# A 128-byte tile ahead of the MLP pool, one rotation step bound to VectorE, and a short VectorE pause at the second half of the token turns

## The chip, the cores and the metric

One Trainium2 chip (trn2), one core of it. The metric is device time in microseconds (us) for one execution of the whole program; the kernel before takes 616.29 us (median of three runs, 615.42 to 616.64). The engines are named as the profile names them: PE (TensorE matmul) and PEld (its weight load), DVE (VectorE), ACT (ScalarE), POOL (GpSimd), SP (SyncE, which issues most transfers).

## What is computed

A two-layer decoder trunk on 256 tokens of width 1024, in float32:

```
for layer in range(2):
    hn = rms_norm(h, gain[layer, 0])
    h = h + (stick_breaking_attention(hn) if layer == 0 else nsa_attention(hn, shared))
    h = h + square(relu(rms_norm(h, gain[layer, 1]) @ w1)) @ w2      # 1024 -> 4096 -> 1024
    if layer == 0:
        shared = nsa_shared_kv(h)        # compressed, selected and window keys and values
return rms_norm(h, final_norm)
```

Layer 0 attends over all earlier tokens with stick-breaking weights. Layer 1 is a native sparse attention: 16 query heads in four groups read compressed blocks, selected blocks and a window, mixed by sigmoid gates. A partial rotary embedding turns the first 16 of each head's 64 query dimensions; the rotated queries are needed for two of the three branches.

## The kernel before, in words

**Precision.** A float32 product is made of three matmuls: each operand is held as a high part (type fp32r) and a low part, and `mm3` (on top of `mm`, whose line is L443) adds high times high, high times low and low times high. For every weight tile of 128x1024 that lands in `raw`, ACT casts it to `wh` (L356) and DVE subtracts to get `wl` (L371). These two are made on the fly for nearly every weight, six buffers deep, and are the largest work of ACT and DVE. In a matmul the first operand in the code is the stationary one (loaded by PEld), the second the moving one (streamed). The names in a profile row stand as moving, stationary.

**Stages.** `layer0` (attention A), `mlp` for layer 0, `layer1` (shared keys and values, queries, sparse attention, output projection), `mlp` for layer 1, then the final norm. Each stage's private tiles live in a tile pool of its own (`ap`), opened by `scoped` at the same place in SBUF; long-lived tiles, the weight buffers (`wp`) and the slots that stages share (`cp`) lie below it.

**MLP.** `mlp` walks the 4096 hidden columns in 16 chunks of 256. For each half of a chunk, `first` multiplies the tokens with w1 into a bank `pu` (eight matmuls of 512 columns with `wh` stationary, eight of 256 with `wl` stationary; the tokens `xn` move). `square` makes the squared ReLU in `ms`, casts it to `hh` (L650) and subtracts to get `hl` (L651). Two chunks later `half` multiplies with w2 into seven accumulators `acc` (512 columns each; here `hh` or `hl` is stationary and the weight moves). Six chunks of each layer use a scheme with fewer products, for which DVE forms sums of weight tiles (`ty`) that are split like the weights into `th` and `tl`; those then move in place of `wh` and `wl`. `ms`, `hh`, `hl`, `th` and `tl` are the tiles of the MLP pool.

**Token turns.** Ahead of each MLP the residual `hres` is transposed on PE into two banks `pt` (`xt_turn`), eight token blocks in two halves of four. `xt_evac` takes each block out: ACT writes the high part of `xn` (L504), DVE the low part (L505). `first` needs block k before its k-th matmul. The second half is turned inside `mlp`, after the first quarter of the first chunk's matmuls.

**Queries of layer 1.** `q_proj` projects one of four groups into a bank `qp`. ACT copies it to `qu` (L1233), DVE multiplies by the cosine table into `qm` (L1234) and shuffles `qu` into `qw` (L1236); then `qw` is multiplied by the sine table (L1237 on POOL or L1238 on DVE) and added to `qm` (L1239 or L1240).

**What sets the order.** PE's instructions stand as the code emits them. The order on DVE, ACT and POOL is made while the kernel is built, by the class `Order`: a planner with its own clock that advances with every matmul. Work comes as chains of steps, each with a rank and, for every engine that may take it, a planned cost. When the planner thinks that an engine is free, it gives it the ready step of lowest rank. `rank_of` gives weight splits 0.5, 2 or 4 by how soon they are used. `quiet` makes an engine take no step of rank 2 or more for a planned time. On the chip each engine then runs its list strictly in order, and waits on semaphores.

**Addresses.** The build gives these tiles the following first bytes in every partition (several buffers of one name differ by 4096, 4608 or 8192 bytes, or by multiples of them, so one stands for all; `xn` has two places):

| tile | role in matmuls | first byte | remainder by 256 |
| --- | --- | --- | --- |
| `wh`, `wl` | moving or stationary | 98208, 122784 | 160 |
| `xa`, `xn`, `xk`, `xq`, `oT` | moving or stationary | 16032 or 49056 | 160 |
| `hh`, `hl` | stationary | 165408, 177696 | 32 |
| `th`, `tl` | moving | 189984, 206368 | 32 |
| `wgs` (layer 1, gate weights) | stationary | 157536 | 96 |

Of the kernel before, what the change touches and what calls it, by code (L numbers as in the profile page):

```python
# [8 lines left out]
F32 = mybir.dt.float32  # L9
# [6 lines left out]
P = 128  # L16
D = 1024
# [141 lines left out]
def act(n, f, more=0):  # L159
    return {"A": (195 + 0.835 * n + more, f, False)}  # L160


def dve(n, f, more=0, port=False):
    return {"D": (150 + 1.045 * n + more, f, port)}
# [7 lines left out]
def hybrid_kernel(ctx, tc, x, xt, eye, gcols, gfin, wqk, wv, wo0, wkv, wvs, wq, wg, wo1, w1, w2, cw1, cw2, cpos, gate_b, consts, out):  # L172
    nc = tc.nc
# [7 lines left out]
    o = Order()  # L181

    def go(gen, rank=1, lag=LAG):
        return Chain(o, gen, rank, o.now + lag)
# [3 lines left out]
    def f32(a):  # L188
        return a.bitcast(F32)

    def slot(i, shape, dt, name):
        return cp.tile(shape, dt, tag=f"e{i}", name=name, bufs=1)
# [4 lines left out]
    def B(i, name, dt=F32):  # L197
        return ps.tile([P, 512], dt, tag=f"b{i}", name=name, bufs=1)
# [215 lines left out]
    def W(i, part=None):  # L414
        if i > ws.cur:
            ws.cur = i
            for q in range(i, min(i + 4, len(items))):
                for c in ws.parts[q] or ():
                    c.hurry(rank_of(q))
        while any(ws.parts[q] is None for q in range(i + 1)):  # L420
            o.run(o.run(o.t))
        for p in range(items[i][3]) if part is None else (part,):
            for q in range(items[i][4] + p + 1):
                c = ws.parts[home[q]][q - items[home[q]][4]]
                if not c.done:
                    c.hurry()
            o.need(ws.parts[i][p])
        return ws.raws[items[i][2][0]] if items[i][0] == "r" else ws.made[i]

    def gone(x):  # L430
        for i in x if isinstance(x, list) else [x]:
            assert ws.gone == i, (ws.gone, i)
            ws.gone += 1
            if items[i][0] == "r":
                used(items[i][2][0])
        now, ws.waiting = ws.waiting, []
        for w in now:
            o.at(o.now, w.finish)
# [10 lines left out]
    def mm3(o_, a, b, first, last):  # L449
        mm(o_, a[0], b[0], first, False)  # L450
        mm(o_, a[0], b[1], False, False)
        mm(o_, a[1], b[0], False, last)

    def tr(o_, a, i, rate=2.0):
        nc.tensor.transpose(o_, a, i)  # L455
        o.tick(a.shape[0] / 2.4 * rate + 3)
# [4 lines left out]
    def both(xt_, k):  # L461
        return xt_[0][:, k, :], xt_[1][:, k, :]

    def cut(hl, a, b):
        return hl[0][:, a:b], hl[1][:, a:b]
# [30 lines left out]
    def xt_banks(banks):  # L496
        return [B(banks[b], f"pt{b}").rearrange("p (j q) -> p j q", j=2) for b in range(2)]

    def xt_evac(pt, j, b, half, gi, xt_, rank=0.5):
        k = 4 * half + 2 * b + j  # L500
        g = gc[:, gi * NK + k:gi * NK + k + 1]

        def one():
            yield act(256, lambda: nc.scalar.activation(xt_[0][:, k, :], pt[b][:, j, :], AF.Copy, scale=g), 60)  # L504
            yield dve(256, lambda: nc.vector.scalar_tensor_tensor(  # L505
                xt_[1][:, k, :], pt[b][:, j, :], g, f32(xt_[0][:, k, :]), op0=OP.mult, op1=OP.subtract), 60)
        return go(one(), rank)

    def xt_turn(pt, half, gi, xt_):
        ch = []  # L510
        for b in range(2):
            for j in range(2):
                k = 4 * half + 2 * b + j
                for t in range(T):
                    tr(pt[b][:, j, t * P:(t + 1) * P], hres[t][:, k * P:(k + 1) * P], ident)
            ch += [xt_evac(pt, j, b, half, gi, xt_) for j in range(2)]
        return ch
# [35 lines left out]
    def mlp(layer, gi, x_, ch, pt, rs, pus, accs, extra, mid, order, ends, ap):  # L553

        ws.tp = ap
        mus = slot(1, [P, 2, 2, 512], F32, "mu")
        mu = [mus[:, i] for i in range(2)]
        wa, wb = i_m[layer]
# [42 lines left out]
        def begin(c):  # L601
            return ([B(pus[c % 2][f], f"pu{f}") for f in range(2)] if c < 4 else [None, None],
                    (mu[c % 2], ap.tile([P, 9, P], F32, name="ms")), [])
# [70 lines left out]
            first(0, st[0], f, 0, NK // 2)  # L674
        gone(wa[0][0])
        o.need(*rs)
        ch.extend(xt_turn(pt, 1, gi, x_))
        st.append(begin(1))
        for f in range(2):
# [315 lines left out]
    def layer1(xk, pt0, ch, ap):  # L995
# [63 lines left out]
        def kv_proj(n, banks, mid=None):  # L1059
            pk = [B(b, "pk") for b in banks]  # L1060
            for k in range(NK):
                if k == 4 and mid is not None:
                    mid()
                if n == 0 and k == 2:
                    o.need(*nxt[2], *nxt[3])
                    pt1 = xt_banks((6, 7))
                    ch.extend(xt_turn(pt1, 1, 4, xk))
                    rc.extend([go(rstd_of(t, rstd), 0.8) for t in range(T)])
                    for half in range(2):
                        for b in range(2):  # L1070
                            for j in range(2):
                                qc[4 * half + 2 * b + j] = xt_evac((pt0, pt1)[half], j, b, half, 2, xq, 2.5)
                w = W(i_kv[n][k // 4][k % 4 // 2])
                if n == 0:
                    o.need(ch[k])
                for t in range(T):
                    mm3(pk[t], tok(xk, k, t), cut(w, k % 2 * 512, (k % 2 + 1) * 512), k == 0, k == NK - 1)
                if k % 2:
                    gone(i_kv[n][k // 4][k % 4 // 2])
            o.need(*rc)  # L1080
            for t in range(T):
                if n == 0:
                    kd0c.append(go(first_out(t, pk[t])))
                else:
                    krope[t] = go(key_out(t, pk[t]), 0.9)
# [125 lines left out]
        def q_proj(g, b, k0=0, k1=NK):  # L1211
            if k0 == 0:
                qps[g] = B(b, "qp")
            qp = qps[g]
            for k in range(k0, k1):
                w = W(i_q[g][k // 4])
                for j in range(2):
                    c = k % 4 * 256 + j * P
                    o.need(qc[k])
                    mm3(qp[:, j * 256:(j + 1) * 256], cut(w, c, c + P), both(xq, k), j == 0 and k == 0, k == NK - 1)  # L1220
                if k % 4 == 3:
                    gone(i_q[g][k // 4])
            if k1 < NK:
                return

            def gen():
                u = ap.tile([P, 2, T * P], F32, name="qu", bufs=3)
                m = ap.tile([P, 2, T * P], F32, name="qm", bufs=3)
                s = ap.tile([P, 2, T * P], F32, name="qw")
                src = qp.rearrange("p (j q) -> p j q", j=2)  # L1230
                tab = [rbc_[:, i, None, :].to_broadcast([P, 2, T * P]) for i in range(2)]
                yield rbc
                yield [act(512, lambda: nc.scalar.copy(u, src), -35),  # L1233
                       dve(512, lambda: nc.vector.tensor_mul(m, src, tab[0]))]  # L1234
                qu[g] = u
                yield dve(512, lambda: nc.vector.stream_shuffle(s, u, swap), 50)  # L1236
                yield {"G": (1040, lambda: nc.gpsimd.tensor_mul(s, s, tab[1]), True),  # L1237
                       "D": (690, lambda: nc.vector.tensor_mul(s, s, tab[1]), True)}  # L1238
                yield {"G": (1260, lambda: nc.gpsimd.tensor_add(m, m, s), True),  # L1239
                       "D": (690, lambda: nc.vector.tensor_add(m, m, s), True)}  # L1240
                qs[g] = m
            qch[g] = go(gen(), 0.8)

        qps, pvs = {}, {}
# [322 lines left out]
        pt = xt_banks((6, 7))  # L1567
# [10 lines left out]
    def scoped(f, name, *a, bufs=2):  # L1578
        with tc.tile_pool(name=name, bufs=bufs, reuse_waits="tile") as ap:
            return f(*a, ap)  # L1580

    x1, ch, pt, rs = scoped(layer0, "l0")
    nxt = {}

    def to_nsa(i, t, n, q, c):
# [3 lines left out]
        if i == 2:  # L1589
# [3 lines left out]
            nxt["ch"] = xt_turn(nxt["pt"], 0, 4, nxt["x"])  # L1593

    scoped(mlp, "m0", 0, 1, x1, ch, pt, rs, ((4, 5), (6, 7)), (0, 1, 2, 3), (4, 5, 6), to_nsa, ((0, 0), (1, 0), (1, 1), (0, 1)), [[(0, 512)]] * 4)
    x1, ch, pt, rs = scoped(layer1, "l1", nxt["x"], nxt["pt"], nxt["ch"], bufs=1)
    gf = slot(0, [P, D], F32, "gf")
# [6 lines left out]
    def finish(i, t, n, q, c):  # L1604
# [37 lines left out]
        last[t].append(go(gen(), 0.2))  # L1642

    scoped(mlp, "m1", 1, 3, x1, ch, pt, rs, ((2, 3), (6, 7)), (0, 1, 4, 5), (2, 3, 6), finish, ((0, 0), (1, 1), (0, 1), (1, 0)), ends)
    o.need(*last[0], *last[1])

# [103 lines left out]
```

## Time and profile before

| | |
| --- | --- |
| runs | 615.42, 616.29, 616.64 us; median 616.29 |
| the profiled execution | 616.42 us, of which the trace's span is 614.6 us |
| granted TensorE clock | 0.997 of full |
| PE busy | 604.0 us (98%), 3544 instructions |
| DVE, ACT, POOL busy | 507.2 us (83%), 377.1 us (61%), 40.6 us (7%) |
| chain that ended last | PE 90%, DVE 5%, DMA 2%, ACT 1%, issue 1% |
| DMA | 108.30 MB, mean 176 GB/s |

How to read it. A matmul's own length in a row (392 ns for 512 columns) is not what it costs, because matmuls overlap; what one costs is the distance from its start to the next start, or the length of a merged piece in the chain of waits divided by its count. "Idle before" stands in brackets in a timeline row, with what ended it. The stages lie at about 0 to 112 us (layer 0's attention), 112 to 288 (its MLP), 288 to 431 (layer 1's shared parts, queries, attention and projection), 431 to 606 (its MLP) and the last 8 us (the final norm's tail).

### The profile page before, as it was taken

Reading aid. Unit: us, or ns where it says so; the run is one execution under the profiler, and the core shown is the slowest. Engines: PE = TensorE matmul, PEld = TensorE weight load, DVE = VectorE, ACT = ScalarE, POOL = GpSimd, SP = SyncE. Lnnn points to the kernel's source line nnn. Section 1 sums busy time; section 2 is a strip of 40 time slices with the busy share of each in tenths; the row PEclk is TensorE's granted clock in tenths of the full one; section 3 lists DMA queues with packets and bytes.
Section 4 is the critical chain, followed back from the end, with each engine's and each line's share of the span. In section 5 each row is a group of like instructions: output and inputs, shape, how many; then the busy total and the mean of one; then the engine's idle time right before and its main releaser. Section 6 shows DMA issues by size and latency. Waiting matters only on the chain.

```text
span 614.6 us, 9427 instructions
## 1 busy us (share of the span) xinstructions
PE 604.0 (98%) x3544; PEld 507.7 (83%) x3544; DVE 507.2 (83%) x743; ACT 377.1 (61%) x623; POOL 40.6 (7%) x57
## 2 busy tenths in 40 slices
PE   8999999999999999999999999999999999999994
PEld 5899988888888888888887888677888888888884
DVE  6669996699889888986837999673997988988885
ACT  6757665566666566664806876462866756656642
POOL 0000000000000000000112442310000000000000
PEclk9999999999999999999999999999999999999998
DMA  8984444274574666565556544223656456465501
GB/s 313 394 275 138 138 134 137 75 262 158 179 245 148 210 203 191 186 231 170 173 170 206 174 145 163 69 70 103 213 164 228 149 193 235 155 209 202 172 0 70
DMA packets 31582, 108.30 MB, mean 176 GB/s; under 512 B 3888, under 2 KB 5168, under 8 KB 31536
## 3 DMA queue, kind: packets, MB, share of 16 engines
q1 hardware_dynamic: 30960, 107.07, 52.2%
q8 instruction: 28, 0.46, 0.3%
q10 hardware_dynamic: 576, 0.62, 0.3%
q14 instruction: 18, 0.15, 0.1%
HBM read 106.63 MB, written 1.05 MB: 175 GB/s over the span
## 4 chain that ended last, share of the span: by engine, by line
PE 90%; DVE 5%; DMA 2%; ACT 1%; issue 1%; POOL 0%; SPq 0%; POOLq 0%; ACTq 0%; DVEq 0%
PE acc L443 35%; PE pu L443 29%; PE qk L443 8%; PE pk L443 4%; PE pv L443 3%; PE po L443 3%; PE z L443 2%; PE qp L443 2%; DVE wl L371 2%; PE ph L443 1%; DMA raw<-in_wq 1%; PE pt L455 1%; PE pa L455 1%; DMA rv<-in_wv 1%; PE ptp L455 1%
## 5 line engine op out<-in xcount | busy, mean ns | idle before, releaser
L371 DVE TENSOR_TENSOR wl<-raw,wh 128x1024 fp32r<-128x1024 f32 (+1 forms) x180 | 210.0, 1190 | 30.9 <-ACT wh L356 29.4
L356 ACT CAST wh<-raw 128x1024 fp32r<-128x1024 f32 (+1 forms) x180 | 180.2, 1025 | 63.5 <-issue 23.2
L443 PE MATMUL pu<-xn,wh 128*128 128x512 f32 x512 | 129.8, 392 | 0.0
L443 PEld LDWEIGHTS pu<-xn,wh 128*128 128x128 f32 x512 | 94.8, 188 | 20.1 <-issue 0.5
L443 PE MATMUL acc<-wh,hl 128*128 128x512 f32 x196 | 77.1, 394 | 0.0
L443 PE MATMUL acc<-wh,hh 128*128 128x512 f32 x196 | 76.9, 393 | 0.0
L443 PE MATMUL acc<-wl,hh 128*128 128x512 f32 x196 | 76.9, 392 | 0.0
L443 PEld LDWEIGHTS pu<-xn,wl 128*128 128x128 f32 x512 | 70.8, 190 | 5.8
L443 PE MATMUL pu<-xn,wl 128*128 128x256 f32 x512 | 72.6, 282 | 0.0
L630 ACT COPY mu<-pu 128x512 f32<-128x512 f32 x64 | 37.3, 583 | 20.8 <-PE pu L443 20.8
L443 PE MATMUL qk<-xa,wh 128*128 128x256 f32 x256 | 47.3, 286 | 0.0
L650 ACT CAST hh<-ms 128x512 fp32r<-128x512 f32 x64 | 34.1, 553 | 16.4 <-DVE ms L646 12.9
L443 PE MATMUL acc<-wh,oT 128*128 128x512 f32 x128 | 43.6, 402 | 0.5 <-DVE oT L533 0.5
L443 PEld LDWEIGHTS acc<-wh,hl 128*128 128x128 f32 x196 | 36.8, 188 | 8.4
L443 PEld LDWEIGHTS acc<-wh,hh 128*128 128x128 f32 x196 | 37.1, 189 | 6.3
L443 PEld LDWEIGHTS acc<-wl,hh 128*128 128x128 f32 x196 | 36.9, 188 | 6.3
L356 ACT CAST th<-ty 128x1024 fp32r<-128x1024 f32 x24 | 25.2, 1051 | 26.2 <-DVE ty L390 13.8
L443 PEld LDWEIGHTS qk<-xa,wh 128*128 128x128 f32 x256 | 39.8, 192 | 0.5 <-issue 0.3
L651 DVE TENSOR_TENSOR hl<-ms,hh 128x512 fp32r<-128x512 f32 x64 | 37.3, 600 | 0.2 <-ACT hh L650 0.2
L443 PE MATMUL qk<-xa,wl 128*128 128x256 f32 x128 | 36.2, 283 | 0.0
L1276 ACT ACTIVATE pe<-z,nm 128x256 f32<-128x256 f32 (+1 forms) x64 | 26.3, 430 | 13.4 <-DVE nm L1282 10.2
L443 PE MATMUL pk<-wh,xk 128*128 128x512 f32 (+1 forms) x128 | 33.6, 342 | 0.0
(202 smaller groups left out, 949.2 us busy)
## 6 DMA issues: line engine op xcount, KB each, us to landing
raw<-in_w SPq DMA_DIRECT2D x128, 512.0 KB, 4.8
raw<-in_wqk SPq DMA_DIRECT2D x16, 512.0 KB, 5.8
raw<-in_wo SPq DMA_DIRECT2D x16, 512.0 KB, 4.2
raw<-in_wkv SPq DMA_DIRECT2D x8, 512.0 KB, 4.8
raw<-in_cw SPq DMA_DIRECT2D x8, 512.0 KB, 4.5
raw<-in_wq SPq DMA_DIRECT2D x8, 512.0 KB, 6.0
rv<-in_wv SPq DMA_DIRECT2D x6, 512.0 KB, 6.9
raw<-in_wvs SPq DMA_DIRECT2D x4, 512.0 KB, 5.7
```

What stands on the lines that cost most here:

```text
L356: k = {"A": (195 + 0.835 * m, lambda: nc.scalar.copy(a, b), False), "D": (200 + 0.49 * m, lambda: nc.vector.tensor_copy(a, b), True)}
L371: yield {"D": (150 + 1.045 * m, lambda: nc.vector.tensor_sub(lo, raw, f32(hi)), True)}
L443: nc.tensor.matmul(o_, a, b, start=first, stop=last, skip_group_check=True)
L455: nc.tensor.transpose(o_, a, i)
L630: yield act(512, lambda: nc.scalar.copy(u[:, f, :], pu[f]))
L650: yield act((b - a) * P, lambda: nc.scalar.copy(hh[:, into], flat[:, q]))
L651: yield dve((b - a) * P, lambda: nc.vector.tensor_sub(hl[:, into], flat[:, q], f32(hh[:, into])), port=True)
L1276: return act(n, lambda: nc.scalar.activation(d, z, AF.Exp, bias=nm[:, i:i + 1], accum_out=rs[:, t, hd, b:b + 1]), 150)
```

## The change

Four edits, of which the second and the last act on the same place:

1. `mlp` first allocates an unused tile of 128 bytes per partition, so that `ms`, `hh`, `hl`, `th` and `tl` all start 128 bytes later. Their remainder by 256 becomes 160, that of the other matmul operands.
2. `xt_evac` gets rank 0.3 instead of 0.5 where no rank is given.
3. In `q_proj` the multiplication by the sine table may no longer go to POOL for the last group (g = 3).
4. In `mlp`, just before the second half of the token turns, `quiet("D", 2200)` keeps DVE free of steps of rank 2 or more for 2200 planned ns.

```diff
-    def xt_evac(pt, j, b, half, gi, xt_, rank=0.5):
+    def xt_evac(pt, j, b, half, gi, xt_, rank=0.3):
...
         ws.tp = ap
+        ap.tile([P, 32], F32, name="pad", bufs=1)
         mus = slot(1, [P, 2, 2, 512], F32, "mu")
...
         o.need(*rs)
+        o.quiet("D", 2200)
         ch.extend(xt_turn(pt, 1, gi, x_))
...
-                yield {"G": (1040, lambda: nc.gpsimd.tensor_mul(s, s, tab[1]), True),
-                       "D": (690, lambda: nc.vector.tensor_mul(s, s, tab[1]), True)}
+                turned = {"G": (1040, lambda: nc.gpsimd.tensor_mul(s, s, tab[1]), True),
+                          "D": (690, lambda: nc.vector.tensor_mul(s, s, tab[1]), True)}
+                yield turned if g < 3 else {"D": turned["D"]}
```

PE's order, its shapes and its operands are the same before and after, and so is SP's order of transfers. What moves is on DVE, ACT and POOL, in three places.

DVE at the second half of the token turns in layer 1's MLP, before (`xn` rows are the low parts of four token blocks; `wl_4481` and `wl_4496` belong to the third chunk, `wl_4412` and `wl_4471` to the first two):

```order
L371 TENSOR_TENSOR wl_4412<-raw_4008,wh_4411 128x1024
L371 TENSOR_TENSOR wl_4471<-raw_4022,wh_4470 128x1024
L371 TENSOR_TENSOR wl_4481<-raw_4233,wh_4480 128x1024
L371 TENSOR_TENSOR wl_4496<-raw_4244,wh_4495 128x1024
L505 SCALAR_TENSOR_TENSOR xn_4417<-pt0_4447,gc_70,xn_4417 128x256 x2
L505 SCALAR_TENSOR_TENSOR xn_4417<-pt1_4448,gc_70,xn_4417 128x256 x2
L371 TENSOR_TENSOR wl_4513<-raw_4363,wh_4512 128x1024
```

The same place after the change (numbers of buffers have moved by one or two):

```order
L371 TENSOR_TENSOR wl_4413<-raw_4009,wh_4412 128x1024
L371 TENSOR_TENSOR wl_4473<-raw_4023,wh_4472 128x1024
L505 SCALAR_TENSOR_TENSOR xn_4418<-pt0_4448,gc_70,xn_4418 128x256 x2
L505 SCALAR_TENSOR_TENSOR xn_4418<-pt1_4449,gc_70,xn_4418 128x256 x2
L371 TENSOR_TENSOR wl_4483<-raw_4234,wh_4482 128x1024
L371 TENSOR_TENSOR wl_4498<-raw_4245,wh_4497 128x1024
L371 TENSOR_TENSOR wl_4514<-raw_4364,wh_4513 128x1024
```

Two weight splits have moved from ahead of the four `xn` steps to behind them. In layer 0's MLP one split moves in the same way. Some later steps of the third and fourth chunk change places with their neighbours in layer 1 (the difference `ms` of 256 columns, its cast and its subtraction go behind a weight split or two); a few rows further on the lists are the same again.

DVE at the last query group, before (`sct` is a step of the compressed branch, `nm` the row maxima of the next head pair, `oT` the attention output that the projection needs):

```order
L1236 STREAM_SHUFFLE qw_3985<-qu_3983 128x512
L371 TENSOR_TENSOR wl_3989<-raw_3799,wh_3988 128x1024
L1240 TENSOR_TENSOR qm_3984<-qm_3984,qw_3985 128x512
L533 TENSOR_TENSOR oT_3991<-po_3992,oT_3991 128x512
L1282 TENSOR_REDUCE nm_4037<-z1_4024 128x2
L1282 TENSOR_REDUCE nm_4037<-z1_4025 128x2
L1422 TENSOR_TENSOR sct_4050<-psc_4044,cst_74 128x256
```

The same place after the change:

```order
L1238 STREAM_SHUFFLE qw_3986<-qu_3984 128x512
L371 TENSOR_TENSOR wl_3990<-raw_3800,wh_3989 128x1024
L1240 TENSOR_TENSOR qw_3986<-qw_3986,rbc_2940 128x512
L1243 TENSOR_TENSOR qm_3985<-qm_3985,qw_3986 128x512
L533 TENSOR_TENSOR oT_3992<-po_3993,oT_3992 128x512
L1285 TENSOR_REDUCE nm_4038<-z1_4025 128x2
L1285 TENSOR_REDUCE nm_4038<-z1_4026 128x2
L1425 TENSOR_TENSOR sct_4051<-psc_4045,cst_74 128x256
```

DVE has one step more, between the split and the addition (lines after the change stand one to three higher). POOL's list loses that step, `L1237 TENSOR_TENSOR qw_3985<-qw_3985,rbc_2939 128x512`, and nothing else.

## The prediction, as it was written before the changed kernel ran

> **What bounds the kernel now.** I read the page's shares first, then the chain of waits.
>
> ```profile
> span 614.6 us, 9427 instructions
> PE 604.0 (98%) x3544; PEld 507.7 (83%) x3544; DVE 507.2 (83%) x743; ACT 377.1 (61%) x623; POOL 40.6 (7%) x57
> PE 90%; DVE 5%; DMA 2%; ACT 1%; issue 1%; POOL 0%; SPq 0%; POOLq 0%; ACTq 0%; DVEq 0%
> ```
>
> The end is set by PE: it is never long idle, and 90% of the chain is its own work. So only two things shorten the run: a smaller distance between matmuls, or a stall of PE taken away. The 5% of DVE are such stalls, nearly all in layer 1's attention.
>
> A matmul's distance is read from merged pieces of the chain (start, length, what; length divided by count). In order of time: 256-column matmuls of layer 0, one steady round of layer 0's MLP (two chunks), then three later places.
>
> ```profile
> 28.40 14.39 PE qk L443 x120
> ...
> 179.89 2.09 PE acc L443 x9
> 181.98 2.77 PE pu L443 x16
> 184.75 2.77 PE acc L443 x12
> 187.53 2.77 PE pu L443 x16
> 190.29 2.77 PE acc L443 x12
> 193.07 2.77 PE pu L443 x16
> 195.83 2.79 PE acc L443 x12
> 198.62 2.81 PE pu L443 x16
> ...
> 294.87 13.65 PE pk L443 x60
> ...
> 326.03 1.85 PE gp L443 x8
> ...
> 411.43 5.49 PE acc L443 x24
> ...
> 460.84 5.58 PE acc L443 x24
> ```
>
> A 256-column matmul takes 119.9 ns (14.39/120). The four `pu` pieces hold 32 matmuls of 512 and 32 of 256 columns in 11.12 us, so one of 512 takes (11.12/32) - 0.120 = 227.6 ns. `pk` takes 227.5 ns. But the four `acc` pieces of the same round hold 45 matmuls in 10.42 us: **231.6 ns**, and the 24 at 460.84 take 232.5. They have the same columns and types, and like `pk` the moving weights `wh` and `wl`. What differs is the stationary tile: `hh` and `hl`, at remainder 32 by 256 in the address table, where `pu` and `pk` have only tiles at 160. Two more pieces fit this. `gp` has a stationary tile at 96 and takes 231.3 ns. The 24 at 411.43 are also called `acc`, but their stationary tile is `oT` at 160: 228.8 ns, a restart behind a transposition included.
>
> **Part 1, the pad.** It moves `hh`, `hl`, `th` and `tl` to 160. How many matmuls touch them, from the groups by form (the first group stands three times with the same count, for `hh`, `hl` and both weight parts; the second too):
>
> ```profile
> L443 PE MATMUL acc<-wh,hl 128*128 128x512 f32 x194 | 76.6, 395 | 0.0
> L443 PE MATMUL acc<-th,hl 128*128 128x512 f32 x48 | 18.9, 394 | 0.0
> ```
>
> 3 x 194 + 3 x 48 = 726. (The 12 of 256 columns at the end gain nothing that I count.) If each falls from 231.6 to the 227.6 of its neighbours `pu`, that is 4.0 ns x 726 = **2.9 us**. Upper end: from the 232.5 of the piece at 460.84 to 227.5, 5.0 x 726 = 3.6 us. Lower end while the address is the cause: to the 228.8 of `oT`, 2.8 x 726 = 2.0 us. If it is not the cause: 0, or less than nothing (rivals). I take 2.9, since `pu` runs in the same rounds beside the same DVE and ACT work.
>
> One thing speaks against the words "share one remainder". `th` and `hh` share one already, 32:
>
> ```profile
> 153.76 0.40 PE L443 MATMUL acc<-wh,hl 128*128 128x512 f32 x1
> 154.00 0.40 PE L443 MATMUL acc<-th,hh 128*128 128x512 f32 x1
> ...
> 155.39 1.78 PE L443 MATMUL pu<-xn,wh 128*128 128x512 f32 x7
> ```
>
> Six matmuls with `th` or `tl` moving in 1.39 us are 231.7 ns each, no less than the mixed ones, and the step from `wh` to `th` took 240. So equality alone does not bring 227.6; 160 together with 160 does. That is enough here, since the change brings all to 160.
>
> The Trainium skill says otherwise: "TensorE: Matmul & The Clock Gate", section "Step-by-step: what each phase is for", gives PE two independent read ports of SBUF, one for the streamed operand and one for weights, and "SBUF — State Buffer", section "SBUF: two separate sides", lets PE wait on nobody. By that rule no start address would cost time, and this part would give 0 (the first rival's sum). The rows of `gp` and `acc` speak against it; that the address is the cause no run here shows yet.
>
> DVE and ACT also read and write the shifted tiles. I count nothing: DVE's subtraction takes 683 ns on `hl` (all at 32) and 679 on `wl` (all at 160).
>
> ```profile
> L651 DVE TENSOR_TENSOR hl<-ms,hh 128x512 fp32r<-128x512 f32 x44 | 30.0, 683 | 0.2 <-ACT hh L650 0.2
> L371 DVE TENSOR_TENSOR wl<-raw,wh 128x512 fp32r<-128x512 f32 x12 | 8.2, 679 | 0.0
> ```
>
> Can the rest follow a faster PE? In the next round (stretch, its length, then busy us of PE, PEld, DVE, ACT, POOL) DVE works 19.27 of 21.53 us, so it has 2.26 free; PE would gain 45 x 4 ns = 0.18. It can.
>
> ```profile
> 201.43:222.96 21.53, 21.53 (x110) 18.27 (x110) 19.27 (x25) 13.68 (x19) 0.00 (x0) 1.00 0.60 196
> ```
>
> **Part 2, the rotation on DVE.** The timeline at the last query group:
>
> ```profile
> 383.76 1.21 DVE L371 TENSOR_TENSOR wl<-raw,wh 128x1024 fp32r<-128x1024 f32 x1
> ...
> 383.95 2.15 POOL L1237 TENSOR_TENSOR qw<-qw,rbc 128x512 f32<-128x512 f32 x1 [3.58 <-DVE qw L1236]
> ...
> 386.13 0.69 DVE L1240 TENSOR_TENSOR qm<-qm,qw 128x512 f32<-128x512 f32 x1 [1.16 <-POOL qw L1237]
> 386.28 0.66 PE L455 MATMUL ptp<-ident,pe 128*128 128x128 f32 x4
> 386.74 0.68 DVE L533 TENSOR_TENSOR oT<-po,oT 128x512 fp32r<-128x512 f32 x1
> ...
> 387.48 0.50 PE L443 MATMUL acc<-wh,oT 128*128 128x512 f32 x1 [0.54 <-DVE oT L533]
> ```
>
> POOL needs 2.15 us, DVE stands idle for 1.16 of it, and behind the waiting addition stands the `oT` subtraction that PE waits for. After the change DVE does the multiplication itself, at the 0.69 us of the addition, which has the same shape. The split ends at 384.97, so the addition starts at about 385.68 instead of 386.13, and `oT` comes 0.45 earlier, at 386.97 instead of 387.42. PE's four transpositions are done at 386.94 (386.28 + 0.66), so PE can take that: **0.45 us**. What comes next on DVE (row maxima, `sct`) feeds ACT and PE in turn and moves along with it. Upper end: PE's whole wait, 0.54. Lower end: 0, if the next wait is not DVE's; below nothing only if POOL was a help, and it was what all waited for.
>
> **Part 3, rank and pause.** The timeline in layer 1's MLP:
>
> ```profile
> 432.61 4.62 DVE L371 TENSOR_TENSOR wl<-raw,wh 128x1024 fp32r<-128x1024 f32 x4
> ...
> 434.66 1.57 ACT L504 ACTIVATE xn<-pt,gc 128x256 fp32r<-128x256 f32 x4 [0.34 <-PE pt L455]
> ...
> 436.31 1.08 PE L443 MATMUL pu<-xn,wh 128*128 128x512 f32 x4
> ...
> 437.15 1.65 DVE L505 SCALAR_TENSOR_TENSOR xn<-pt,gc,xn 128x256 fp32r<-128x256 f32 x4
> ...
> 437.71 1.71 PE L443 MATMUL pu<-xn,wh 128*128 128x512 f32 x4
> ...
> 439.73 1.08 PE L443 MATMUL pu<-xn,wh 128*128 128x512 f32 x4
> ...
> 445.76 1.11 PE L443 MATMUL pu<-xn,wl 128*128 128x256 f32 x8
> ```
>
> From 436.31 to 437.71 a group of four and four takes 1.40 us; the next one takes 2.02 (437.71 to 439.73), because its second to fourth matmul wait for the low parts that DVE makes only from 437.15 on, behind four splits. The stall is **0.62 us**. After the change two splits stand ahead; DVE is free at 432.61 + 4.62/2 = 434.9, the first high part is there at 435.1, and four low parts at DVE's pace (1.65 us) end by 436.8, before PE asks for the first at 437.71. The whole stall goes. What is late next: the two splits that moved back end by about 439.1, the later one's use comes after the use of the earlier one at 445.76. That is over 6 us of cover. DVE stands idle for about 0.2 us more, which its free time above takes.
>
> In layer 0 the same place has no stall, so the pause gives and costs nothing there:
>
> ```profile
> 120.12 1.65 DVE L505 SCALAR_TENSOR_TENSOR xn<-pt,gc,xn 128x256 fp32r<-128x256 f32 x4
> ...
> 121.86 1.09 PE L443 MATMUL pu<-xn,wh 128*128 128x512 f32 x4
> ```
>
> DVE is done with the low parts at 121.77 when PE starts on them at 121.86.
>
> **Sum.** 2.9 + 0.45 + 0.62 = 4.0 us. Against the profiled execution's own 616.42 us (span 614.6) that gives 612.4. This execution stands 0.13 above the median of 616.29, so the forecast for a median is **612.4**, the difference being below what I can resolve. With the ends of the parts (2.0 + 0 + 0.62 and 3.6 + 0.54 + 0.62) its own range is 611.5 to 613.7.
>
> **The rivals.**
>
> *The address is not the cause.* Then `acc` stays at 231.6 and only parts 2 and 3 remain: 616.3 - 1.1 = 615.2. For it: only two of my pieces have the same output name and differ in the remainder, and `th` with `hh` takes 231.7 though equal. Against it: five kinds of pieces sort themselves by 160 or not, in three stages. Chance 0.13.
>
> *The pad works, but the DVE gains are swallowed.* PE in layer 1's attention goes from one wait to the next, so 0.45 may end in another wait, and the MLP's head in the next late split. Then 616.3 - 2.9 = 613.4. Against it: the splits behind have more than 6 us of cover. Chance 0.10.
>
> *Equal remainders collide (slower).* The one equal pair that is not at 160, `th` with `hh`, takes 231.7 ns, and the step into it took 240. If weight loads and streaming from one remainder hindered each other, all 726 would go to 240: 8.4 x 726 = 6.1 us more, less 1.1, 621.3. It decides from 1.5 ns a matmul on (1.1 us / 726), where it has eaten the other gains. Against it: `pk`, `pu` and `oT` have 160 in both operands and take the least. Chance 0.05.
>
> **How the numbers follow.** Forecast 0.72, the rivals 0.13, 0.10 and 0.05. Differences below 0.2% (1.2 us) cannot be told from none here. Faster: the forecast, the second rival, and a quarter of the first, which lies at the bound: 0.85. Same: the rest of the first, 0.10. Slower: 0.05. The range leaves out the collision and the thin ends: 611.4 to 615.3.
>
> **What would show it.** Step by step: in the chain after, `acc` x12 pieces of 2.73 instead of 2.77 to 2.79 us, and x24 pieces of 5.46 to 5.48 instead of 5.58. At the rotation, no idle time of DVE ahead of the addition, and PE's wait for `oT` near 0.1. In layer 1's MLP, groups of `pu` of 1.40 us throughout. DVE's and ACT's mean times on `hl` and `hh` unchanged. The prediction is wrong if `acc` stays at 231 ns, if `pu` or `pk` (untouched) change too, or if a new wait of PE on DVE's `wl` shows near 440 to 450 us.

## The result, and the profile after

| | before | after |
| --- | --- | --- |
| median of the runs | 616.15 us (615.42 to 616.64) | 611.45 us (611.15 to 611.62) |
| the profiled execution | 616.42 us, span 614.6 | 611.62 us, span 609.9 |
| PE busy | 604.0 us | 601.1 us |

The ratio is 0.9924, with a 95% interval of 0.9907 to 0.9941: 4.7 us less, where 4.0 were forecast (612.4); the median lies just inside the low end of the range, 611.4. The page's shares after the change:

```profile
PE 601.1 (99%) x3544; PEld 508.2 (83%) x3544; DVE 508.0 (83%) x744; ACT 376.9 (62%) x623; POOL 38.6 (6%) x56
PE 94%; DVE 3%; DMA 1%; ACT 1%; issue 1%; POOLq 0%; POOL 0%; DVEq 0%; ACTq 0%
```

The matmuls' busy time has shrunk by 2.9 us, and DVE's part of the chain has gone from 5% to 3%. The chain of waits (start, length, what) at the places that the prediction showed:

```profile
28.01 14.39 PE qk L443 x120
...
186.57 2.77 PE pu L443 x16
189.33 2.75 PE acc L443 x12
...
194.85 2.75 PE acc L443 x12
197.59 2.77 PE pu L443 x16
...
292.98 13.65 PE pk L443 x60
...
324.14 1.85 PE gp L443 x8
...
408.77 5.49 PE acc L443 x24
...
457.47 5.47 PE acc L443 x24
```

The pieces of `acc` with `hh` and `hl`, the products with the squared ReLU, are called the squares from here on. They have become shorter: `acc` x12 takes 2.75 us instead of 2.77 to 2.79, x24 takes 5.47 instead of 5.58. `pk` (13.65), `gp` (1.85) and the x24 with `oT` (5.49), whose tiles the change does not move, are the same to the hundredth. And the `pu` piece behind the `th` block, 2.81 before, is 2.77 now, although its own operands, `xn` and `wh`, stand where they stood.

The timeline at the last query group (start, busy us, and in brackets the idle time ahead):

```profile
382.76 0.69 DVE L1240 TENSOR_TENSOR qw<-qw,rbc 128x512 f32<-128x512 f32 x1
383.48 0.69 DVE L1243 TENSOR_TENSOR qm<-qm,qw 128x512 f32<-128x512 f32 x1
384.09 0.68 DVE L533 TENSOR_TENSOR oT<-po,oT 128x512 fp32r<-128x512 f32 x1
384.16 0.66 PE L455 MATMUL ptp<-ident,pe 128*128 128x128 f32 x4
384.83 0.50 PE L443 MATMUL acc<-wh,oT 128*128 128x512 f32 x1
384.83 0.19 PEld L443 LDWEIGHTS acc<-wh,oT 128*128 128x128 f32 x1 [0.25 <-DVE oT L533]
```

DVE now multiplies `qw` itself and goes on to the addition without idle time. `oT` is done at 384.77 (384.09 + 0.68), PE's four transpositions at 384.82 (384.16 + 0.66), and the matmul starts at 384.83: the 0.54 us that PE stood idle ahead of it are gone, and the transpositions are what ends last. The 0.25 in the last row is idle time of the weight load (0.78 at the same row before), which no longer holds PE up. The timeline at the second half of the token turns in layer 1:

```profile
432.90 1.66 DVE L505 SCALAR_TENSOR_TENSOR xn<-pt,gc,xn 128x256 fp32r<-128x256 f32 x4 [0.59 <-ACT xn L504]
...
434.47 4.62 DVE L371 TENSOR_TENSOR wl<-raw,wh 128x1024 fp32r<-128x1024 f32 x4
...
435.07 1.09 PE L443 MATMUL pu<-xn,wh 128*128 128x512 f32 x4
...
436.48 1.09 PE L443 MATMUL pu<-xn,wh 128*128 128x512 f32 x4
```

The low parts of `xn` are made first and the weight splits behind them; DVE waits 0.59 us for ACT's high part, which costs nobody anything, and PE's second group starts 1.41 us behind the first (435.07 to 436.48). The stall of 0.62 us is gone.

**Where the 4.8 us between the two profiled executions went.** The spans hold 4.7 of it. Starts of the same piece in both chains, before minus after: 0.39 us at the first `qk` piece; 1.89 at `pk` (294.87 to 292.98), so layer 0's MLP gave 1.50; 2.66 at the `acc` with `oT` (411.43 to 408.77), so layer 1's front gave 0.77; 3.23 at the first squares of layer 1 (449.67 to 446.44), 0.57 more; and the rest, 1.5, between there and the end, nearly all of it layer 1's MLP. The two MLPs' 3.0 are the pad. Of the 0.77, 0.52 lie between the shuffle and the `acc` behind it (383.15 to 387.48 before, 381.02 to 384.83 after): the rotation. The 0.39 at the start and some 0.2 in layer 1's front lie at places that the change does not touch, and are looked at below.

### The profile page after: what moved, and what is told of

It is laid out like the page before. It is cut to its first block, busy times and chain, and to the rows that moved or that the text cites. A ratio compares the mean times of both kernels' runs of the same rounds, so it can differ in the third digit from the quotient of the medians.

```text
span 609.9 us, 9427 instructions
## 1 busy us (share of the span) xinstructions
PE 601.1 (99%) x3544; PEld 508.2 (83%) x3544; DVE 508.0 (83%) x744; ACT 376.9 (62%) x623; POOL 38.6 (6%) x56
## 4 chain that ended last, share of the span: by engine, by line
PE 94%; DVE 3%; DMA 1%; ACT 1%; issue 1%; POOLq 0%; POOL 0%; DVEq 0%; ACTq 0%
PE acc L443 34%; PE pu L443 29%; PE qk L443 8%; PE pk L443 4%; PE pv L443 4%; PE po L443 3%; PE z L443 3%; PE qp L443 3%; PE ptp L455 1%; PE ph L443 1%; DMA raw<-in_wq 1%; PE pt L455 1%; PE pa L455 1%; DVE wl L371 1%; PE warm L443 1%
## 5 line engine op out<-in xcount | busy, mean ns | idle before, releaser
L443 PE MATMUL pu<-xn,wh 128*128 128x512 f32 x512 | 128.5, 390 | 0.0
L651 ACT CAST hh<-ms 128x512 fp32r<-128x512 f32 (+1 forms) x64 | 34.0, 553 | 17.2 <-DVE ms L647 13.4
L652 DVE TENSOR_TENSOR hl<-ms,hh 128x512 fp32r<-128x512 f32 (+1 forms) x64 | 37.3, 601 | 0.2 <-ACT hh L651 0.2
```

Of the source, the lines that this page charges most:

```text
L443: nc.tensor.matmul(o_, a, b, start=first, stop=last, skip_group_check=True)
L651: yield act((b - a) * P, lambda: nc.scalar.copy(hh[:, into], flat[:, q]))
L652: yield dve((b - a) * P, lambda: nc.vector.tensor_sub(hl[:, into], flat[:, q], f32(hh[:, into])), port=True)
```

## The experiments

Nine kernels vary the addresses or take single edits, one takes the pause away. In all of them each engine issues the same instructions in the same order as the kernel that they are built from, but for the edits named. "An x24 piece" is one of `acc` with `hh` and `hl`, unless `oT` is named. Each run was measured in a session with the kernel before, whose median there lay between 615.91 and 616.15 us; differences to the changed kernel compare medians of different sessions, so their last tenths are not certain.

### The pad alone, and everything but the pad

```diff
+        ap.tile([P, 32], F32, name="pad", bufs=1)     # alone, added to the kernel before
```

> The kernel before with the 128-byte tile alone; DVE, ACT, POOL and PE issue the same rows in the same order as before. Theory A (the start address of the MLP's operands sets the distance of their matmuls): 616.2 - 3.0 = 613.2 us, the four acc x12 pieces of a steady round near 2.74 instead of 2.77 to 2.79, the last x24 piece of layer 1 near 5.47 instead of 5.58; the waits of DVE on qw (1.16 us) and of PE in the pu groups of layer 1 (2.02 us) stay. Theory C (the trace of after has shorter acc pieces for another reason, such as the changed order on DVE): 616.2, acc x24 stays 5.58.

Measured 612.6 us; ratio to before 0.9951 (0.9939 to 0.9964), 3.0 us, with an interval of 2.2 to 3.8 (3.4 between the medians, 615.99 before in that session). Its chain has the piece lengths of the kernel after, and the stall of layer 1 is still there: `pu` x80 holds it and takes 14.60 us, where the kernel after has 14.02.

```profile
194.67 2.75 PE acc L443 x12
...
197.42 2.77 PE pu L443 x16
...
432.76 14.60 PE pu L443 x80
...
458.39 5.47 PE acc L443 x24
```

The other way round, the rotation, the rank and the pause without the pad:

```diff
-        ap.tile([P, 32], F32, name="pad", bufs=1)     # taken out of the changed kernel
```

> The changed kernel without the 128-byte tile: rotation, rank and pause alone. Theory A: 616.2 - 0.53 - 0.61 = 615.1 us; acc x24 pieces at 5.58, no idle time of DVE ahead of the qm addition, PE's wait for oT 0.25, pu groups of 1.40. If the 0.6 us by which the two traces differ ahead of any changed work (0.39 us at the first qk piece, 0.21 in the start of layer 1) hang on the DVE and POOL edits, 614.5. Theory C: near the changed kernel, 611.5 to 612.5, with acc x24 at 5.47.

Measured 614.57 us, ratio 0.9978 (0.9969 to 0.9986), 1.4 us. Its x24 pieces are back at 5.58, its x80 piece at 14.02.

```profile
434.02 14.02 PE pu L443 x80
...
459.20 5.58 PE acc L443 x24
```

Theory C (another reason than the address) is out: the shorter pieces come and go with the pad, and with nothing else. The two gains, 3.4 and 1.4 between medians, add up to 4.8, near the 4.7 of the whole, so no sign is seen that the parts disturb each other (the interval of the first alone is 1.6 us wide).

### Is it the address, or that the tiles moved?

```diff
-        ap.tile([P, 32], F32, name="pad", bufs=1)     # 128 bytes
+        ap.tile([P, 64], F32, name="pad", bufs=1)     # 256 bytes, added to the kernel before
```

> The kernel before with an unused tile of 256 bytes instead of 128, so that the five tiles move but stay at remainder 32. Theory A with the remainder by 256 as what counts: 616.2 us, acc x24 at 5.58, x12 at 2.77 to 2.79. Rival: moving the tiles at all (another distance to the tiles below them, or a coarser part of the address) gives the gain: 613.2, acc x24 at 5.47.

Measured 615.6 us, ratio 0.9995 (0.9986 to 1.0004): no difference. The pieces are those of the kernel before, to the 2.79 and 2.81 around the `th` block:

```profile
27.70 14.39 PE qk L443 x120
...
195.13 2.79 PE acc L443 x12
197.92 2.81 PE pu L443 x16
...
459.93 5.58 PE acc L443 x24
```

So 256 bytes more do nothing, 128 bytes more give 3 us. What counts seems to repeat every 256 bytes. (With the pad of 128 bytes `hh` starts at 165536 and `wh` at 98208, which differ by an odd number of 256 bytes; so equality by 512 is not needed.)

### 160, or the same for all?

```diff
     npow = cp.tile([P, 1], F32, name="npow")
+    cp.tile([P, 32], F32, name="low", bufs=1)         # added to the changed kernel
```

> The changed kernel with a second unused tile of 128 bytes below all matmul operands: wh, wl, xa, xn, xk, xq, oT, hh, hl, th and tl all start at remainder 32 by 256 (wgs at 224). Theory B (the operands must share one remainder, whichever it is): 611.5 us as the changed kernel, pu x16 2.77, pk x60 13.65, acc x24 5.47. Theory A (160 is a good start and 32 a bad one, shared or not): every matmul of 512 columns near 231.6 ns, 1600 x 4.0 = 6.4 us more, 617.9 us; pu x16 2.83, pk x60 13.90, acc x24 5.57; what the matmuls of 256 columns do is open, they are not counted.

Measured 611.55 us, ratio 0.9929 (0.9915 to 0.9942): the time of the changed kernel.

```profile
183.57 2.75 PE acc L443 x12
186.32 2.77 PE pu L443 x16
...
292.71 13.63 PE pk L443 x60
...
458.12 5.47 PE acc L443 x24
```

Theory B stands and theory A of this expectation (160 good, 32 bad) falls: remainder 32 is as good as 160, if all share it. That is against a step of the prediction, which read from the `th` block (32 with 32, 231.7 ns) that equality alone would not do.

### Weights on one side, tokens on the other

```diff
+    wp.tile([P, 32], F32, name="low", bufs=1)         # ahead of raw, wh, wl; added to the changed kernel
```

> The changed kernel with a second unused tile of 128 bytes ahead of raw, wh and wl: these three and hh, hl, th, tl at remainder 32; xa, xn, xk, xq and oT stay at 160. Theory B: the squares of the MLP stay as fast as in the changed kernel (wh with hh are equal: acc x24 5.47, x12 2.75), but everything that has tokens or oT on one side and weights on the other is mixed: some 870 matmuls of 512 columns, 4.0 ns each, 3.5 us more, 615.0 us; eight pu of 512 and eight of 256 columns 2.80 instead of 2.77, pk x60 13.88 instead of 13.65, acc<-oT x24 5.58. Rival (only the tiles of the MLP pool matter, for instance because DVE and ACT write them while PE reads): pu, pk and acc unchanged, 611.5.

Measured 615.99 us, ratio 1.0 (0.999 to 1.0009): the whole gain is lost, 4.5 us against the changed kernel (4.4 in PE's busy time, 605.5 against 601.1), where theory B had said 3.5. (In this kernel the matmul line is L444.)

```profile
28.54 14.39 PE qk L444 x120
...
193.46 2.81 PE pu L444 x16
196.28 2.77 PE acc L444 x12
...
295.38 13.95 PE pk L444 x60
...
411.53 5.58 PE acc L444 x24
...
460.44 5.46 PE acc L444 x24
```

The sides have changed places, as theory B said: `pu` 2.81, `pk` 13.95 and the x24 with `oT` 5.58 are the slow ones now, and the long piece of squares, with `wh` and `hh` both at 32, is fast with 5.46. The rival, that only the MLP pool's tiles matter because DVE and ACT write them meanwhile, falls: `pk` has none of them, and has slowed by 0.30. What theory B missed are the short pieces of squares: their operands are equal, yet x12 takes 2.77, not 2.75. And one thing does not slow at all: the 120 matmuls of `qk` have the tokens `xa` at 160 and the weights at 32 here, and take 14.39 us as in every other run. They move 256 columns, not 512; the loss is seen only at 512.

### Which operand: moving alone, stationary alone

```diff
         # th alone at 32: an unused tile of 128 bytes between hl and th, the pad stays
+        if ws.between is not ws.tp:
+            ws.between = ws.tp
+            ws.tp.tile([P, 32], F32, name="between", bufs=1)
```

> The changed kernel with a second unused tile of 128 bytes between hl and th: ms, hh and hl at remainder 160, th and tl (moving) alone at 32. Theory B (a matmul of 512 columns takes 4 ns more when its moving and its stationary tile differ in the remainder, each matmul for itself): only the 144 with th or tl moving are mixed, 144 x 4.0 = 0.6 us more than the changed kernel, 612.1 us; acc x24 stays 5.47, pu x16 stays 2.77 behind the blocks with th too. Theory H (the moving tile's change of remainder leaves PE off its rhythm for several matmuls, whatever the stationary tile is): the step from wh to th near 239 instead of 227.5, the six of th near 231.9 instead of 227.7, and the pu group behind them 2.81, together 61 ns in each of 24 blocks, 1.5 us more, 613.0 us.

Measured 612.49 us, ratio 0.9945 (0.993 to 0.996), 1.0 us over the changed kernel. In the chain (line L447 here) only the pieces with `th` are longer, and the `pu` behind them takes 2.78:

```profile
194.64 2.78 PE acc L447 x12
197.42 2.78 PE pu L447 x16
```

The trace's starts give 227.5 ns for the step from `wh` to `th` (theory H: 239), 230.9 in the block (both theories: 231.6 to 231.9), and behind it 231.3, 229.6 and 228.8 for the first three of `pu`, then 226.7. Theory B has the size nearly right, and it misses the three. The times alone would not decide between its 612.1 us and the 613.0 of theory H: the four runs lie between 612.00 and 613.26.

```diff
         # hh and hl alone at 32: the same unused tile, the pad ahead of ms taken out
-        ap.tile([P, 32], F32, name="pad", bufs=1)
```

> The changed kernel with the unused tile between hl and th instead of ahead of ms: ms, hh and hl (stationary) at remainder 32, th and tl at 160. Theory B: all 726 matmuls of 512 columns with hh or hl are mixed, 2.9 us more than the changed kernel, 614.4 us; acc x24 5.58, th blocks near 231.6, and (what is only seen here) no more than that in the step from wh to th and in the pu group behind th, 2.77 instead of 2.81. Theory H alone (only a change of the moving tile's remainder costs): 611.5 us, acc x24 5.47, since every moving tile is at 160.

Measured 614.04 us, ratio 0.9969 (0.9958 to 0.9981), 2.6 us over the changed kernel. The chain (line L447):

```profile
195.14 2.77 PE acc L447 x12
197.91 2.77 PE pu L447 x16
...
458.62 5.58 PE acc L447 x24
```

Theory H (only a change of the moving tile costs) falls with the 5.58: no moving tile has changed here. Theory B said 2.77 for the `pu` behind the `th` block, which holds, and 2.9 us in all, which is a little much. The pair of `th` and `hh` is unequal in both runs: its mean is 230.9 ns where the moving tile was shifted and 231.6 where the stationary one was, so either shift costs much the same.

### Is near enough?

```diff
-        ap.tile([P, 32], F32, name="pad", bufs=1)
+        ap.tile([P, 24], F32, name="pad", bufs=1)     # 96 bytes: hh, hl, th, tl at 128
```

> The changed kernel with an unused tile of 96 bytes instead of 128: hh, hl, th and tl at remainder 128, 32 bytes away from that of wh, wl and xn. If the remainders must be equal: as without the tile, 614.5 us, acc x24 5.58. If being near is enough, or what counts is which half of 256 bytes a tile starts in: 611.5 us, acc x24 5.47. If the cost grows with the distance (32 of 128): a quarter of 3.0 us, 612.3, acc x24 5.50.

Measured 615.96 us, ratio 0.9996 (0.9987 to 1.0006), 4.5 us over the changed kernel (PE's busy time 605.5, 4.4 more): 32 bytes beside the others (on the low side, the only one tried) cost more than 128 bytes beside them.

```profile
196.23 2.79 PE acc L443 x12
199.02 2.79 PE pu L443 x16
...
435.42 14.02 PE pu L443 x80
...
460.62 5.60 PE acc L443 x24
```

```diff
-        ap.tile([P, 32], F32, name="pad", bufs=1)
+        ap.tile([P, 16], F32, name="pad", bufs=1)     # 64 bytes: hh, hl, th, tl at 96
```

> The changed kernel with an unused tile of 64 bytes instead of 128: hh, hl, th and tl at remainder 96, 64 bytes from the 160 of the others. If any inequality costs the same: like the run with 96 bytes, 616.0 us, with 5.60 for the acc x24 pieces. If the distance between the remainders sets the size (5.60 was measured at a distance of 32 bytes, 5.58 at 128, 5.47 at 0): between, 5.58 to 5.60, 614.5 to 616.0 us. If 64 is again a good distance: 611.5 us, 5.47. The eight gp matmuls, whose stationary tile wgs stands at 96, took 231 ns and speak against the last.

Measured 613.51 us, ratio 0.9958 (0.9943 to 0.9973), 2.1 us over the changed kernel.

```profile
192.71 2.79 PE pu L443 x16
195.50 2.76 PE acc L443 x12
...
458.65 5.49 PE acc L443 x24
```

None of the three expectations fits whole. The x24 piece is nearly fast (5.49), and most of the loss stands in `pu`, 2.79, whose operands are equal. Near is not enough, and the cost does not grow with the distance: 32 bytes cost 4.5 us, 64 cost 2.1, 128 cost 3.1 (614.57 against 611.45).

### The sequence behind it

Why do matmuls with equal operands pay in the last three cases? The starts of successive matmuls of 512 columns, in ns from one to the next, in one round of layer 0's MLP (six with `wh` and `wl`, six with `th` and `tl`, then, after a bar, eight of `pu`; sixteen of 256 columns and more lie between rounds; the same row returns in all twelve rounds of this form in both MLPs, each number within 1 ns):

```
before     231 232 228 230 232 241 239 233 236 224 231 231 | 235 233 236 224 231 236 228 232
after      233 236 228 233 231 226 227 227 226 227 227 226 | 227 227 226 227 227 226 227 227
weights 32 236 233 236 224 231 236 228 233 230 227 227 226 | 235 224 237 229 238 229 238 229
pad 96     229 235 233 235 230 235 230 236 229 232 231 235 | 230 224 231 236 228 233 230 227
pad 64     226 229 232 226 229 231 231 236 228 233 231 226 | 228 229 233 236 224 231 236 228
```

The distances are not noise, they are patterns. With equal remainders there is one row of numbers, 233 236 224 231 236 228 233 230 (in the line "weights 32" ahead of the bar), which is entered at some point, sometimes with a skip, and ends in a steady 226.7 (227 227 226 over and over). Of all distances of 512 columns, 70% are 226 or 227 in the kernel after, 34% in the one before. Between unequal remainders it does not come to that: they have other patterns, such as 226 229 232 with 64 bytes between them (a mean of 229, hence the 5.49). In the line "weights 32" the first part (equal) gets there after nine matmuls, and the `pu` behind it (unequal) comes to alternate between 229 and 238. What is left of the disorder is paid by the equal pairs that come next, as `pu` does in the last two lines, until the row is run through or the group ends. In the line "before", the `th` block and the `pu` behind it are both equal pairs: both run through much of the row, but six and eight matmuls are not enough to reach its end. That is why `th` with `hh` looked slow, and why `pu` took 2.81 there. An unequal row need not leave disorder: behind twelve squares with `wh` and `wl`, all unequal, the `pu` of the kernel before runs at 227 227 226 from its first step. So it matters where in its pattern the unequal row stops. The same in means over all matmuls of 512 columns (distances of 260 ns and more, which are stalls, left out):

| kernel | remainder of weights, tokens, `hh`, `th` | `pu` | `acc` with `hh`, `hl` | with `th`, `tl` | `pk` | us |
| --- | --- | --- | --- | --- | --- | --- |
| before | 160, 160, 32, 32 | 229.0 | 231.9 | 231.9 | 227.6 | 616.15 |
| after | 160, 160, 160, 160 | 227.7 | 228.9 | 227.5 | 227.6 | 611.45 |
| all at 32 | 32, 32, 32, 32 | 227.6 | 228.9 | 227.5 | 227.5 | 611.55 |
| `th` at 32 | 160, 160, 160, 32 | 228.2 | 228.9 | 230.9 | 227.6 | 612.49 |
| `hh` at 32 | 160, 160, 32, 160 | 228.1 | 231.7 | 231.6 | 227.6 | 614.04 |
| weights at 32 | 32, 160, 32, 32 | 232.4 | 229.8 | 229.4 | 232.4 | 615.99 |
| pad of 96 | 160, 160, 128, 128 | 230.5 | 233.1 | 232.1 | 227.6 | 615.96 |
| pad of 64 | 160, 160, 96, 96 | 230.2 | 228.9 | 230.7 | 227.7 | 613.51 |

`pk` is never preceded by squares of the MLP, and it keeps 227.6 wherever its own pair is equal. The `pu` x80 piece, ahead of the first squares, is 13.99 to 14.03 in all of them that have no stall, with weights and tokens unequal too (14.03): behind the transpositions it runs unsteadily even with equal operands (most of its distances are between 224 and 236 there in the kernel after), so it has little to lose. What in the hardware holds this memory from one matmul to the next is not settled; no run here looks inside PE or its reads.

### The pause

```diff
-        o.quiet("D", 2200)                            # taken out of the changed kernel, rank 0.3 stays
```

> The changed kernel without the pause (tile, rotation and rank 0.3 stay). DVE's list at the token turns is then the one of the kernel before, so the rank alone moves nothing. Theory of the prediction: the stall of PE in layer 1's MLP is back, the second pu group takes 2.02 instead of 1.41 us, 0.61 us more, 612.1 us; layer 0 unchanged. Rival (the stall's time is anyway lost in a later wait on weights): 611.5 us with the 2.02 group, and a wait of PE that the changed kernel has between 440 and 450 us is gone.

Measured 612.35 us, ratio 0.9941 (0.9928 to 0.9953), 0.9 us over the changed kernel, with runs that spread by as much (611.73 to 612.89). The trace is sharper:

```profile
430.36 4.62 DVE L371 TENSOR_TENSOR wl<-raw,wh 128x1024 fp32r<-128x1024 f32 x4
...
434.90 1.65 DVE L505 SCALAR_TENSOR_TENSOR xn<-pt,gc,xn 128x256 fp32r<-128x256 f32 x4
...
435.47 1.69 PE L443 MATMUL pu<-xn,wh 128*128 128x512 f32 x4
...
437.47 1.08 PE L443 MATMUL pu<-xn,wh 128*128 128x512 f32 x4
```

The second group takes 2.00 us (435.47 to 437.47) instead of 1.41. From the `acc` with `oT` to the first squares of layer 1 this kernel takes 38.26 us (409.17 to 447.43), the changed one 37.67 (408.77 to 446.44): 0.59. From there to the last x60 piece both take the same, 139.26 and 139.27, so nothing is given back, and the rival falls. The rank alone moves nothing: DVE's list at this place is that of the kernel before, and the kernel as built with the rank left at 0.5 and the pause kept (no run was made of it) has the lists of the changed kernel on all engines, row for row. The pause is the whole of part 3.

## Why the prediction was right, point by point

**What bounds.** Right: every part that shortened PE's spacing or a stall of PE came out in the end time.

**The pad, 2.9 us.** Right in size: 1.50 in each MLP, 3.0 in all, 2.9 in PE's busy time. It came in another split than the sum had it. The 726 matmuls were to fall from 231.6 to 227.6 ns; those with `hh` and `hl` and the weights fell from 231.9 to 228.9 (3.0 x 582 = 1.7 us), those with `th` from 231.9 to 227.5 (4.4 x 144 = 0.6), and `pu`, counted at nothing, from 229.0 to 227.7 (1.3 x 510 = 0.7). That the total came out is in part luck: the squares gave 2.4 us where the sum had 2.9, and `pu` filled the gap. The prediction's own sign "wrong if `pu` or `pk` change too" has come true for `pu`, behind the `th` blocks: that only the matmuls with a shifted tile would change was wrong.

**The step that failed** is the reading "equality alone does not bring 227.6; 160 together with 160 does". With all at 32 the time is 611.55 us. The `th` block, on which the step rested, is six matmuls behind an unequal row, too short to become steady; a mean over it says nothing of its own pair. The same holds for `gp`, which the prediction took as support: its 1.85 us are eight matmuls behind transpositions, and an equal group of eight in the unsteady `pu` x80 piece of the kernel after (from 127.09 us) runs at 235 233 236 224 231 236 228 232, no faster. The forecast survived since the change makes all equal.

By the two independent read ports of the Trainium skill ("TensorE: Matmul & The Clock Gate", section "Step-by-step: what each phase is for") the pad would have given 0; the pad alone measures 3.0 us in the traces. The number of ports is not thereby refuted, but spacing does hang on where both operands start.

**The rotation, 0.45 us.** 0.52 measured. The term was mis-sized because it took the split's row at its full length; rows on DVE overlap, and the split of 1.21 us is followed by the multiplication after 1.12 (it starts at 381.64, the multiplication at 382.76). So `oT` came 0.52 earlier against the shuffle, and the transpositions, which the prediction named as the next limit, became it: PE's idle time ahead of the matmul is 0.01, where near 0.1 was forecast.

**Rank and pause, 0.62 us.** 0.57 to 0.59 in the chain, 0.61 in the group itself; the rank has no part in it. In layer 0 the x80 piece is 14.01 before and after: nothing, as said. DVE's free time did take the 0.59 of idling, where 0.2 was forecast. No new wait on `wl` shows: `pu` x80 (432.42 to 446.44) goes over into the first squares without a gap.

**The costs at nothing.** DVE's subtraction on the moved tiles takes 684 ns (683 before), ACT's cast 620 (620).

```profile
L652 DVE TENSOR_TENSOR hl<-ms,hh 128x512 fp32r<-128x512 f32 x44 | 30.1, 684 | 0.2 <-ACT hh L651 0.2
L651 ACT CAST hh<-ms 128x512 fp32r<-128x512 f32 x44 | 27.3, 620 | 16.9 <-DVE ms L647 13.4 <-DVE ms L663 3.5
```

**The rivals.** "The address is not the cause" falls with the pad alone, "swallowed" with the pause taken out and with the sum of the parts, "equal remainders collide" with all at 32.

**The rest.** The parts come to 3.0 + 0.52 + 0.59 = 4.1 of the 4.8 between the profiled executions. The rest is put down to scatter: the first `qk` piece, ahead of which no experiment but the two that move weights and tokens changes anything that PE reads, starts between 27.65 and 28.54 us in the twelve profiles, and the kernel with the pad of 256 bytes, which has the order of the kernel before, has it at 27.70 against 28.40. From `gp` to the `acc` with `oT` the kernel before takes 85.40 us, and the two kernels with its order, the pad alone and the pad of 256 bytes, take 85.15 and 85.17. So about half a microsecond of the measured 4.7 may be luck, probably of when transfers landed (no run isolates that), which the interval allows: it runs from 3.6 us (0.0059 of 616) to 5.7 (0.0093).

## What to carry to other kernels

In a kernel that PE bounds with matmuls of 512 columns (type fp32r here, weights loaded anew for each; no other type was tried), look up the start addresses of all matmul operands, and bring moving and stationary tiles to one remainder by 256 bytes: here 32 did as well as 160, a near miss of 32 bytes was the worst of the three distances tried, and the price is 128 bytes. Read a matmul's spacing from a long uniform run, and ask what stood ahead of a short one, since six matmuls still carried the disorder of the row ahead of them. A stall of PE on an engine that is only 83% busy is an order in its list: move what PE needs next ahead of what it needs later, and check that the gain is still there at the next three pieces.

## What the runs showed that was not expected

- The spacing of matmuls of 512 columns has a steady state of 226.7 ns and a fixed row of numbers between 224 and 236 that leads to it within some nine matmuls if the operands' remainders are equal. In the kernel after, each row of squares still begins with about five such steps (233 236 228 233 231), behind the matmuls of 256 columns. That is what keeps `acc` at 228.9.
- Matmuls of 256 columns lose nothing: with weights at 32 and tokens at 160 the 120 of `qk` take 14.39 us, as with both at 160.
- The cost of unequal remainders is not monotone in their distance: 4.5, 2.1 and 3.1 us for 32, 64 and 128 bytes.
- An unused tile of 128 bytes below all operands, which moves every one of them, changes nothing (611.55 us), and below the weights alone it costs 4.5 us.
